# Twenty-four weight units get their high part by a converting transfer on GpSimd's queue, where VectorE copied it before

## The chip, the cores and the metric

The kernel runs on one core of a Trainium2 chip. The metric is the device time of one execution in microseconds, the median of several runs.

## The reference, cut to what matters

Two layers, each of a half-step feed-forward block, a mixer and a second half-step feed-forward block, on 256 tokens of width 1024 in fp32:

```
for l in range(2):
    x = x + 0.5 * swiglu(rmsnorm(x, ffn1_norm[l]), ffn1_w_up[l], ffn1_w_down[l])   # 1024 -> 2*2816 -> 1024
    p = rmsnorm(x, mix_norm[l]) @ w_in[l]
    p_rwkv, p_ga, p_wa, p_gate = split(p)             # 1920, 768, 768 and 3*1024 columns
    y_a = rwkv_mixer(p_rwkv, ...)                     # a scan over the tokens in both directions
    y_b = global_attention(...)                       # from p_ga
    y_c = window_attention(...)                       # from p_wa
    g = sigmoid(p_gate)                               # three gates of 1024
    merged = g0 * (y_a @ w_o_rwkv[l]) + g1 * (y_b @ w_o_ga[l]) + g2 * (y_c @ w_o_wa[l])
    x = x + merged @ w_out[l]
    x = x + 0.5 * swiglu(rmsnorm(x, ffn2_norm[l]), ffn2_w_up[l], ffn2_w_down[l])
return rmsnorm(x, final_norm)
```

## The kernel before

**Weights in units.** Every large matmul works on weight units of 128x1024 fp32 numbers (512 KB), made by `unit()`. A unit is loaded into `w_raw` by SyncE's queue (L80, three buffers). Its high part `w_hi` is the copy that rounds to fp32r (L91, four buffers): on ScalarE this copy is recorded at L61, on VectorE, as a CAST, at L63. Its low part `w_lo` is raw minus high (L92, four buffers), on VectorE or on GpSimd. Activations are held as a high and a low part too, and `mm3` makes each product from three matmuls: high by high, high by `w_lo`, and low by high. All these matmuls stand at L51, so the profile tells them apart by their output: `up` and `dn` in the feed-forward blocks, and in the mixer `pj` (queries, keys and values), `rk` (RWKV projections), `gt` (gates) and `wo` (output projections).

**Who makes which part.** In the feed-forward blocks ScalarE makes the high part and VectorE the low part. In the mixer the string `ENG` has a letter per unit for the engine pair: `v` ScalarE and VectorE, `p` ScalarE and GpSimd, `w` VectorE and GpSimd, `x` VectorE for both. `Mixer.on` turns the letter into the pair. Kind Q is the projection of queries, keys and values (12 units), R the RWKV projections, F the gates and the three output projections. In each layer twelve units have an `x`: Q1, Q2, Q3 and Q6, R6, and F3, F12, F13, F22 (of `w_o_wa`), F26, F32 and F33 (both of `w_o_rwkv`).

**The mixer's order.** The string `ORDER` interleaves generators: Q, R and F units, the attention steps, and the chunks of the RWKV scan. A scheduler then sets the order on each engine; each engine works through its own instructions in that order, and an instruction that waits holds up all behind it. Each layer's chunk work has a serial piece on VectorE: products of PSUM with masks (L743, L744: `LAt`, `LRt`), 32-wide transposes (L767), a substitution in pairs of small operations on `sol` (L775, L776: a multiply and an add), and the transpose into `Tn` (L785). TensorE then takes `Tn` to make `gp` and `tp` (32x32 matmuls), `hb`, `bonp` and `gatep`, among which it has `gt` matmuls. The gates' products are added into `merged` at L972 and L973. The RWKV projection is scaled into `RKV` at L611 and L612.

**GpSimd.** At the start of a mixer it makes the norm's statistics (L142 to L145), then issues six small transfers for the attention's constants (L393 to L397), and from these makes tables (L401, L407). Behind them stands its first `w_lo`. Later it makes some 30 `w_lo` per layer and small steps between.

Of the kernel before, what the change touches and what calls it, by code (L numbers as in the profile page):

```python
# [28 lines left out]
class Net:  # L29
# [38 lines left out]
    def unit(self, *srcs, on="av", turn=False):  # L68
        nc = self.nc
        raw = self.wp.tile([128, 1024], F32, name="w_raw", tag="w_raw", bufs=NRAW)  # L70
        c = 0
        for s in srcs:
            shp = s.shape
            n = 1
            for d in shp[1:]:
                n *= d
            dst = raw[:, c:c + n]
            if len(shp) == 3:
                dst = dst.rearrange("p (k c) -> p k c", k=shp[1])
            nc.sync.dma_start(out=dst, in_=s)  # L80
            c += n
        hi = self.wp.tile([128, 1024], F32R, name="w_hi", tag="w_hi", bufs=NHI)
        lo = self.wp.tile([128, 1024], F32R, name="w_lo", tag="w_lo", bufs=NLO)

        for i in range(2 if turn else 1):
            if turn:
                r = raw.rearrange("p (k w d c) -> p k w d c", w=2, d=2, c=64)[:, :, i]
                h, o = (x.rearrange("p (k d w c) -> p k d w c", w=2, d=2, c=64)[:, :, :, i] for x in (hi, lo))
            else:
                r, h, o = raw[:, :c], hi[:, :c], lo[:, :c]  # L90
            self.copy(on[0], h, r)  # L91
            self.engine(on[1]).tensor_tensor(o, r, h.bitcast(F32), ALU.subtract)  # L92
        return hi, lo

# [172 lines left out]


ORDER = 'QQQQQRRQQQRRQAQQRRRAAKAQRRPARRAKRKPVAVAARFRARFPVVAAAAAVAAVFAAFPAPFFVFFV00FFF01FF11F1001F01000000110F01F0F010PF1211F122PFFP112F1O3F32F3FFFO332323O223322F322232FF23323333OOOFFFFF'
ENG = {'Q': 'vxxxvvxppvvv', 'R': 'pvvwvpxvvvvvvvv', 'F': 'ppvxppppppppxxpppwpvvvxwwpxpppppxxwp', 'M': 'vvpvpvvv', 'O': 'vpvvpvvv', 'T': 'vaaaaaaaaaavavaa', 'G': 'vavaaa'}  # L270
KAP = float(np.exp(-0.5))
R_MU, R_W0, R_A0, R_KK, R_KA, R_RK, R_LG, R_LB, R_N = 0, 15, 23, 31, 35, 39, 43, 47, 51
PARTS = [("rwkv_mu", 15), ("rwkv_w0", 8), ("rwkv_a0", 8), ("rwkv_k_k", 4), ("rwkv_k_a", 4), ("rwkv_r_k", 4), ("rwkv_lnx_g", 4), ("rwkv_lnx_b", 4)]
# [15 lines left out]
class Mixer:  # L289
# [48 lines left out]
    def take(self, kind):  # L338
        s = ENG[kind]
        self.nlo[kind] = i = self.nlo.get(kind, -1) + 1  # L340
        return s[i % len(s)]
# [2 lines left out]
        return self.n.engine(self.take(kind))  # L344

    def on(self, kind):
        return {"v": "av", "p": "ap", "w": "vp", "x": "vv"}[self.take(kind)]


    def proj(self, c0, res, kind, first=False):  # L350
# [708 lines left out]
```

## Time and profile before

| | |
|---|---|
| runs | 1503.72, 1504.91 and 1505.63 us, median 1504.91 |
| the profiled execution | 1505.69 us, its span 1503.8 us, mean granted TensorE clock 0.98 |
| TensorE busy | 1425.9 us, 95% of the span |
| VectorE busy | 925.7 us, 62% |
| ScalarE busy | 701.9 us, 47% |
| GpSimd busy | 224.5 us, 15% |
| transfers | 220.19 MB, 146 GB/s over the span |

The mixers run from about 195 to 530 us and from about 940 to 1275 us of the span; the rest is feed-forward work. A time in the trace is counted from the span's start. A row's bracket gives the idle time of the engine ahead of it and what released it. TensorE's busy time includes waiting in its pipeline, so it is read with the gaps beside it.

### The profile page before, as it was taken

How to read it: one execution, taken by the hardware profiler on the slowest of the kernel's cores; microseconds unless marked ns; L12 is line 12 of the kernel's file. 1: busy time of each engine (PE TensorE's matmuls, PEld its weight loads, DVE VectorE, ACT ScalarE, POOL GpSimd, SP SyncE). 2: the span in 40 equal slices, each digit the busy share in tenths (PEclk: the TensorE clock that was granted, in tenths of full speed). 3: DMA queues.
4: the chain of work that ended last, by engine and by line, in shares of the span. 5: the costliest groups of instructions: out<-in, count | busy, mean ns of one | idle time of the engine just before them, and what ended most of it. 6: DMA issues, size and time to landing. Idle time of an engine off the chain costs nothing.

```text
span 1503.8 us, 25092 instructions
## 1 busy us (share of the span) xinstructions
PE 1425.9 (95%) x10170; PEld 1167.8 (78%) x10170; DVE 925.7 (62%) x1384; ACT 701.9 (47%) x1109; POOL 224.5 (15%) x203
## 2 busy tenths in 40 slices
PE   8999999999797999999999999999997979999997
PEld 6888878877575778888888888788785758788886
DVE  5455468765859666555465554778657685755543
ACT  6444335764333246444354443466642332554443
POOL 0000033223214110000000000432242132100001
PEclk9999999999899899999999999999998989999999
DMA  7666656323313146666666666553242121576653
GB/s 220 195 198 189 189 149 187 109 85 106 106 51 98 53 133 182 185 181 190 186 182 184 182 185 193 152 170 105 78 125 87 44 86 58 153 213 182 194 182 112
DMA packets 113432, 220.19 MB, mean 146 GB/s; under 512 B 7362, under 2 KB 32164, under 8 KB 113316
## 3 DMA queue, kind: packets, MB, share of 16 engines
q1 hardware_dynamic: 111328, 215.08, 47.7%
q10 hardware_dynamic: 1508, 2.58, 0.6%
q8 instruction: 80, 1.31, 0.4%
q0 software_dynamic: 480, 0.93, 0.3%
q14 instruction: 36, 0.29, 0.1%
HBM read 217.51 MB, written 1.05 MB: 145 GB/s over the span
## 4 chain that ended last, share of the span: by engine, by line
PE 69%; DVE 14%; issue 5%; ACT 5%; DMA 4%; POOL 3%; SPq 0%; POOLq 0%; ACTq 0%; DVEq 0%
PE up L51 26%; PE dn L51 18%; PE gt L51 5%; DMA w_raw<-in_ffn_w_up 3%; DVE w_lo L92 3%; PE rk L51 3%; PE tp L54 2%; PE wo L51 2%; PE yv L51 2%; ACT w_hi L61 1%; DVE sol L775 1%; PE tx L51 1%; DVE sol L767 1%; DVE sol L776 1%; PE pj L51 1%
## 5 line engine op out<-in xcount | busy, mean ns | idle before, releaser
L92 DVE TENSOR_TENSOR w_lo<-w_raw,w_hi 128x1024 fp32r<-128x1024 f32 (+1 forms) x348 | 427.0, 1229 | 343.3 <-ACT w_hi L61 342.4
L61 ACT ACTIVATE w_hi<-w_raw 128x1024 fp32r<-128x1024 f32 (+1 forms) x376 | 394.6, 1051 | 469.1 <-PE up L51 175.0
L51 PE MATMUL up<-w_hi,hT 128*128 128x512 f32 x1408 | 443.5, 394 | 0.0
L51 PEld LDWEIGHTS up<-w_hi,hT 128*128 128x128 f32 x1408 | 265.3, 189 | 53.9
L51 PE MATMUL up<-w_lo,hT 128*128 128x512 f32 x704 | 274.5, 391 | 0.0
L51 PE MATMUL dn<-w_hi,aT 128*128 128x512 f32 x704 | 218.2, 390 | 0.0
L92 POOL TENSOR_TENSOR w_lo<-w_raw,w_hi 128x1024 fp32r<-128x1024 f32 (+1 forms) x62 | 147.5, 2383 | 228.1 <-ACT w_hi L61 146.1
L51 PEld LDWEIGHTS up<-w_lo,hT 128*128 128x128 f32 x704 | 132.7, 188 | 28.2 <-DVE w_lo L92 1.1
L51 PEld LDWEIGHTS dn<-w_hi,aT 128*128 128x128 f32 x704 | 131.7, 188 | 26.8
L51 PE MATMUL dn<-w_lo,aT 128*128 128x512 f32 x352 | 138.0, 392 | 0.0
L51 PE MATMUL gt<-w_hi,hT 128*128 128x512 f32 x384 | 135.8, 418 | 2.3 <-DVE w_hi L63 2.3
L51 PE MATMUL rk<-hT,w_hi 128*128 128x256 f32 x480 | 88.2, 285 | 2.5 <-DVE RKV L611 2.5
L51 PEld LDWEIGHTS gt<-w_hi,hT 128*128 128x128 f32 x384 | 73.8, 195 | 20.6 <-issue 3.0
L51 PE MATMUL gt<-w_lo,hT 128*128 128x512 f32 x192 | 80.5, 419 | 2.5 <-DVE w_lo L92 2.5
L142 POOL TENSOR_SCALAR stat<-stat 128x1 f32<-128x1 f32 x14 | 3.5, 254 | 511.1 <-ACT gh L138 495.0
L51 PEld LDWEIGHTS rk<-hT,w_hi 128*128 128x128 f32 x480 | 75.3, 191 | 4.4 <-DVE RKV L611 2.9
L51 PEld LDWEIGHTS dn<-w_lo,aT 128*128 128x128 f32 x352 | 66.1, 188 | 14.8 <-DVE w_lo L92 1.4
L51 PE MATMUL rk<-hT,w_lo 128*128 128x256 f32 x240 | 67.9, 284 | 1.4 <-POOL w_lo L92 1.4
L51 PE MATMUL wo<-w_hi,yT 128*128 128x512 f32 x192 | 65.5, 407 | 0.0
L51 PE MATMUL pj<-w_hi,hT 128*128 128x512 f32 x192 | 62.0, 397 | 2.1 <-DVE LG L611 2.1
L51 PEld LDWEIGHTS rk<-hT,w_lo 128*128 128x128 f32 x240 | 45.8, 191 | 1.8 <-POOL w_lo L92 1.8
L51 PEld LDWEIGHTS gt<-w_lo,hT 128*128 128x128 f32 x192 | 37.5, 195 | 11.6 <-DVE w_lo L92 3.2
(238 smaller groups left out, 1833.8 us busy)
## 6 DMA issues: line engine op xcount, KB each, us to landing
w_raw<-in_ffn_w_up SPq DMA_DIRECT2D x160, 512.0 KB
w_raw<-in_w_in SPq DMA_DIRECT2D x102, 512.0 KB
w_raw<-in_ffn_w_down SPq DMA_DIRECT2D x88, 512.0 KB
w_raw<-in_ffn_w_up SPq DMA_DIRECT2D x32, 256.0 KB
w_raw<-in_w_out SPq DMA_DIRECT2D x16, 512.0 KB
w_raw<-in_w_o_ga SPq DMA_DIRECT2D x8, 512.0 KB
w_raw<-in_w_o_wa SPq DMA_DIRECT2D x8, 512.0 KB
w_raw<-in_w_o_rwkv SPq DMA_DIRECT2D x8, 512.0 KB
```

What stands on the lines that cost most here:

```text
L51: return self.nc.tensor.matmul(*a, **k)
L54: return self.nc.tensor.transpose(*a, **k)
L61: self.nc.scalar.activation(out, in_, AF.Copy, scale=1.0 if scale is None else scale)
L92: self.engine(on[1]).tensor_tensor(o, r, h.bitcast(F32), ALU.subtract)
L142: nc.gpsimd.tensor_scalar(self.ss[:, c:c + 1], self.ss[:, c:c + 1], 1.0 / D, EPS, ALU.mult, ALU.add)
L767: V.transpose(sol[p0:p0 + 32], src[p0:p0 + 32, :, 32 * b:32 * b + 32].rearrange("p g (u t) -> p t u g", u=2))
L775: V.tensor_tensor(tv, Dm[:, s + 1:16, s:s + 1].to_broadcast([128, m, s]), Dm[:, s:s + 1, 0:s].to_broadcast([128, m, s]), ALU.mult)
L776: V.tensor_tensor(Dm[:, s + 1:16, 0:s], Dm[:, s + 1:16, 0:s], tv, ALU.add)
```

## The change

A new letter `d` takes the place of `x` at all twelve places per layer, 24 in all. For such a unit, GpSimd issues a second transfer from the same place in DRAM, into `w_hi`, whose type (fp32r) differs from the source's, so that the transfer converts. VectorE's copy of the unit is left out. The low part is made by VectorE as before; it now waits for both transfers. The ten CASTs of letter `w` stay. Each of the new transfers moves 512 KB in 256 runs of 2 KB (128x2x512; R6's in 512 runs of 1 KB), and by the buffers of `w_hi` it waits for the matmuls that read its buffer's last unit. Lines behind the new code stand 8 further down: L92 is now L100.

```
         hi = self.wp.tile([128, 1024], F32R, name="w_hi", tag="w_hi", bufs=NHI)
         lo = self.wp.tile([128, 1024], F32R, name="w_lo", tag="w_lo", bufs=NLO)
+        if on[0] == "d":
+            c = 0
+            for s in srcs:
+                k = s.shape[1]
+                n = k * s.shape[2]
+                nc.gpsimd.dma_start(out=hi[:, c:c + n].rearrange("p (k c) -> p k c", k=k), in_=s)
+                c += n
...
-            self.copy(on[0], h, r)
+            if on[0] != "d":
+                self.copy(on[0], h, r)
             self.engine(on[1]).tensor_tensor(o, r, h.bitcast(F32), ALU.subtract)
...
-ENG = {'Q': 'vxxxvvxppvvv', 'R': 'pvvwvpxvvvvvvvv', 'F': 'ppvxppppppppxxpppwpvvvxwwpxpppppxxwp', ...
+ENG = {'Q': 'vdddvvdppvvv', 'R': 'pvvwvpdvvvvvvvv', 'F': 'ppvdppppppppddpppwpvvvdwwpdpppppddwp', ...
...
-        return {"v": "av", "p": "ap", "w": "vp", "x": "vv"}[self.take(kind)]
+        return {"v": "av", "p": "ap", "w": "vp", "x": "vv", "d": "dv"}[self.take(kind)]
```

**GpSimd at the start of the first mixer.** The norm's steps on `stat` for the second half of the tokens, and the attention's transfers behind them, before:

```order
L145 TENSOR_TENSOR stat_68<-stat_68 128x1
L142 TENSOR_SCALAR stat_68<-stat_68 128x1
L144 TENSOR_SCALAR stat_68<-stat_68 128x1
L145 TENSOR_TENSOR stat_68<-stat_68 128x1
L393 DMA at2_1580<-c_rope 128x2x128
```

and now, where `w_hi_1625`, `w_hi_1637` and `w_hi_1649` are the units Q1, Q2 and Q3:

```order
L153 TENSOR_TENSOR stat_68<-stat_68 128x1
L89 DMA w_hi_1625<-in_w_in 128x2x512
L150 TENSOR_SCALAR stat_68<-stat_68 128x1
L89 DMA w_hi_1637<-in_w_in 128x2x512
L89 DMA w_hi_1649<-in_w_in 128x2x512
L152 TENSOR_SCALAR stat_68<-stat_68 128x1
L153 TENSOR_TENSOR stat_68<-stat_68 128x1
L401 DMA at2_1580<-c_rope 128x2x128
```

The three transfers stand between the norm's steps and ahead of the attention's transfers.

**VectorE ahead of the substitution, first mixer.** `w_hi_4286` and `w_lo_4287` are the parts of unit F26. Before:

```order
L973 TENSOR_TENSOR merged_2937<-merged_2937,gth_4067 128x512
L743 TENSOR_TENSOR LAt_3872<-Lp0_4202,consts_494 128x256
L744 TENSOR_TENSOR LRt_4157<-Lp0_4202,consts_494 128x4x64
L743 TENSOR_TENSOR LAt_3872<-Lp1_4203,consts_494 128x256
L744 TENSOR_TENSOR LRt_4157<-Lp1_4203,consts_494 128x4x64
L63 CAST w_hi_4286<-w_raw_4284 128x1024
L767 STREAM_TRANSPOSE sol_4354<-LAt_3872 32x512
L92 TENSOR_TENSOR w_lo_4287<-w_raw_4284,w_hi_4286 128x1024
L63 COPY LRt_4157<-T1_4246 64x8x64
```

and now:

```order
L981 TENSOR_TENSOR merged_2937<-merged_2937,gth_4067 128x512
L751 TENSOR_TENSOR LAt_3872<-Lp0_4202,consts_494 128x256
L752 TENSOR_TENSOR LRt_4157<-Lp0_4202,consts_494 128x4x64
L751 TENSOR_TENSOR LAt_3872<-Lp1_4203,consts_494 128x256
L752 TENSOR_TENSOR LRt_4157<-Lp1_4203,consts_494 128x4x64
L100 TENSOR_TENSOR w_lo_4287<-w_raw_4284,w_hi_4286 128x1024
L775 STREAM_TRANSPOSE sol_4354<-LAt_3872 32x512
L63 COPY LRt_4157<-T1_4246 64x8x64
```

The CAST is gone and the low part has its place. Likewise the CAST of F32, which stood right ahead of the transposes into `Tn` at the end of the substitution, is gone there, and F32's low part has moved from between `Tn` and its use to behind the step that follows `tp` (L799). GpSimd issues F26's transfer ahead of the `w_lo` that starts at 453.47 us in the trace of before. In the second mixer F26's low part stands at the place of its CAST, four pairs of `LAt` and `LRt` earlier than before.

**TensorE at the use of Tn, first mixer.** `w_lo_4802` and `w_hi_4801` are the parts of another gate unit:

```order
 L51 MATMUL gt0_4699<-w_hi_4801,hT0_65 128x512
+L51 MATMUL gp_4394<-Tn_4392,LAt_3872 32x32 x32
+L51 MATMUL gp_4430<-Tn_4428,LAt_3872 32x32 x32
+L51 MATMUL tp1_4464<-sol_4354,Tn_4392 32x32 x32
+L51 MATMUL tp1_4503<-sol_4354,Tn_4428 32x32 x32
+L54 MATMUL hb_4542<-head_67,pz_4147 128x128 x4
 L51 MATMUL gt0_4699<-w_lo_4802,hT0_65 128x512
 L51 MATMUL gt0_4699<-w_hi_4801,hT1_66 128x512
```

The `gp`, `tp` and `hb` matmuls stand five `gt` matmuls earlier, so these five come behind `hb` now. In the second mixer three are moved so.

## Rows read from the trace of the kernel before

**Rows 1.** The page: busy time by engine, and the chain of work that ended last, by engine.

```profile
PE 1425.9 (95%) x10170; PEld 1167.8 (78%) x10170; DVE 925.7 (62%) x1384; ACT 701.9 (47%) x1109; POOL 224.5 (15%) x203
PE 69%; DVE 14%; issue 5%; ACT 5%; DMA 4%; POOL 3%; SPq 0%; POOLq 0%; ACTq 0%; DVEq 0%
```

**Rows 2.** Busy time of each engine in four stretches: stretch, its length, then busy us (and instructions) of PE, PEld, DVE, ACT and POOL, then the granted clock, the share of the DMA engines and GB/s.

```profile
462.00:490.00 28.00, 19.06 (x137) 14.76 (x129) 26.93 (x55) 8.62 (x11) 14.81 (x7) 0.92 0.36 113
490.00:498.00 8.00, 6.75 (x265) 6.22 (x266) 4.86 (x10) 3.14 (x8) 0.56 (x1) 0.50 0.21 70
1195.00:1225.00 30.00, 24.11 (x205) 18.34 (x204) 28.72 (x57) 8.23 (x11) 14.39 (x7) 0.97 0.34 106
1225.00:1234.00 9.00, 4.56 (x259) 4.39 (x260) 4.93 (x13) 2.54 (x5) 3.76 (x2) 0.50 0.21 62
```

**Rows 3.** VectorE's CASTs at L63: shortest, median and longest in ns, then the first and the last start.

```profile
L63 DVE CAST w_hi<-w_raw x34: 669/693/1977, 200.6 to 1257.3; 128x1024 fp32r<-128x1024 f32 x34
```

**Rows 4.** VectorE's timeline ahead of `Tn` in the first mixer: start, us, what.

```profile
463.92 2.83 DVE L973 TENSOR_TENSOR merged<-merged,gth 128x512 f32<-128x512 f32 x1
...
468.00 1.98 DVE L63 CAST w_hi<-w_raw 128x1024 fp32r<-128x1024 f32 x1
...
470.88 1.17 DVE L92 TENSOR_TENSOR w_lo<-w_raw,w_hi 128x1024 fp32r<-128x1024 f32 x1
...
477.67 2.36 DVE L776 TENSOR_TENSOR sol<-sol 128x36 f32<-128x36 f32 x1
...
480.30 0.20 DVE L776 TENSOR_TENSOR sol<-sol 128x44 f32<-128x44 f32 x1
...
488.92 0.67 DVE L63 CAST w_hi<-w_raw 128x1024 fp32r<-128x1024 f32 x1
```

**Rows 5.** GpSimd's timeline in the same stretch.

```profile
463.82 2.38 POOL L92 TENSOR_TENSOR w_lo<-w_raw,w_hi 128x1024 fp32r<-128x1024 f32 x1 [1.20 <-PE Lp L51]
467.08 2.35 POOL L92 TENSOR_TENSOR w_lo<-w_raw,w_hi 128x1024 fp32r<-128x1024 f32 x1 [0.87 <-ACT w_hi L61]
```

**Rows 6.** TensorE's timeline in the same stretch and up to the use of `Tn`.

```profile
470.04 0.51 PE L51 MATMUL gt<-w_hi,hT 128*128 128x512 f32 x1 [2.27 <-DVE w_hi L63]
472.10 0.79 PE L51 MATMUL gt<-w_lo,hT 128*128 128x512 f32 x1 [1.56 <-DVE w_lo L92]
472.69 1.05 PE L51 MATMUL gt<-w_hi,hT 128*128 128x512 f32 x2
473.55 0.63 PE L51 MATMUL gt<-w_lo,hT 128*128 128x512 f32 x1
...
481.07 0.63 PE L51 MATMUL gt<-w_hi,hT 128*128 128x512 f32 x2
481.54 0.39 PE L51 MATMUL gt<-w_lo,hT 128*128 128x512 f32 x1
...
490.08 1.93 PE L51 MATMUL gp<-Tn,LAt 32*32 32x32 f32 x128 [5.19 <-DVE Tn L785]
```

**Rows 7.** The same place in the second mixer: VectorE's timeline.

```profile
1202.49 1.17 DVE L63 CAST w_hi<-w_raw 128x1024 fp32r<-128x1024 f32 x1
...
1208.19 3.17 DVE L92 TENSOR_TENSOR w_lo<-w_raw,w_hi 128x1024 fp32r<-128x1024 f32 x1
...
1216.87 2.22 DVE L775 TENSOR_TENSOR sol<-sol 128x14 f32<-128x14 f32 x1
```

**Rows 8.** GpSimd's and then TensorE's timeline there.

```profile
1201.45 1.66 POOL L973 TENSOR_TENSOR merged<-merged,gth 128x512 f32<-128x512 f32 x1 [3.22 <-DVE gth L972]
...
1207.89 2.39 POOL L92 TENSOR_TENSOR w_lo<-w_raw,w_hi 128x1024 fp32r<-128x1024 f32 x1 [1.17 <-ACT w_hi L61]
...
1227.83 1.93 PE L51 MATMUL gp<-Tn,LAt 32*32 32x32 f32 x128 [7.42 <-DVE Tn L785]
```

**Rows 9.** The transfers: the queue that carries the weights (packets, MB, share of the 16 engines' span), and the issues from GpSimd's queue (count, KB each, median us from issue to landing).

```profile
q1 hardware_dynamic: 111328, 215.08, 47.7%
...
at<-c_rope POOLq DMA_DIRECT2D x4, 128.0 KB, 2.6
...
at<-in_ga_k_norm POOLq DMA_DIRECT2D x2, 32.0 KB, 5.2
```

**Rows 10.** GpSimd's timeline at the start of the first mixer.

```profile
202.22 0.30 POOL L142 TENSOR_SCALAR stat<-stat 128x1 f32<-128x1 f32 x1 [4.91 <-ACT gh L138]
204.57 0.79 POOL L144 TENSOR_SCALAR stat<-stat 128x1 f32<-128x1 f32 x1 [2.06 <-ACT gh L138]
...
208.04 1.70 POOL L393 DMA_DIRECT2D at<-c_rope  x2 [2.04 <-PE tp L54]
```

**Rows 11.** VectorE's timeline at the start of the first mixer, and at unit R6.

```profile
200.64 0.69 DVE L63 CAST w_hi<-w_raw 128x1024 fp32r<-128x1024 f32 x1 [0.18 <-PE dn L51]
...
204.02 1.21 DVE L92 TENSOR_TENSOR w_lo<-w_raw,w_hi 128x1024 fp32r<-128x1024 f32 x1
...
253.77 0.47 DVE L611 SCALAR_TENSOR_TENSOR RKV<-rk,par,projpad 128x256 f32<-128x256 f32 x1
```

**Rows 12.** TensorE's timeline at the same two places.

```profile
205.29 0.50 PE L51 MATMUL pj<-w_lo,hT 128*128 128x512 f32 x1 [1.11 <-DVE w_lo L92]
...
220.88 0.39 PE L51 MATMUL rk<-hT,w_lo 128*128 128x256 f32 x1 [0.79 <-POOL w_lo L92]
...
254.30 0.50 PE L51 MATMUL rk<-hT,w_hi 128*128 128x256 f32 x2 [1.29 <-DVE RKV L611]
```

More of the change, by code (lines that the diff above doesn't have):

```diff
@@ L269 @@
 ORDER = 'QQQQQRRQQQRRQAQQRRRAAKAQRRPARRAKRKPVAVAARFRARFPVVAAAAAVAAVFAAFPAPFFVFFV00FFF01FF11F1001F01000000110F01F0F010PF1211F122PFFP112F1O3F32F3FFFO332323O223322F322232FF23323333OOOFFFFF'
-ENG = {'Q': 'vxxxvvxppvvv', 'R': 'pvvwvpxvvvvvvvv', 'F': 'ppvxppppppppxxpppwpvvvxwwpxpppppxxwp', 'M': 'vvpvpvvv', 'O': 'vpvvpvvv', 'T': 'vaaaaaaaaaavavaa', 'G': 'vavaaa'}
+ENG = {'Q': 'vdddvvdppvvv', 'R': 'pvvwvpdvvvvvvvv', 'F': 'ppvdppppppppddpppwpvvvdwwpdpppppddwp', 'M': 'vvpvpvvv', 'O': 'vpvvpvvv', 'T': 'vaaaaaaaaaavavaa', 'G': 'vavaaa'}
 KAP = float(np.exp(-0.5))
```

## The prediction

> **What bounds the kernel now.** The page comes first: TensorE is busy 95% of the span, and the chain that ended last is 69% TensorE and 14% VectorE [rows 1]. So a microsecond counts only where TensorE stands idle; VectorE's 34 CASTs, 0.693 us each at the median [rows 3], cost nothing by themselves. Next come the stretches: ahead of the use of `Tn`, TensorE is busy 19.06 of 28 us and VectorE 26.93; in the second mixer VectorE is busy 28.72 of 30 us [rows 2]. There VectorE sets the time. The timelines show how: TensorE waits 5.19 us for `Tn` in the first mixer [rows 6] and 7.42 us in the second [rows 8], and VectorE has hardly a gap before that. Its pieces are of two kinds: work of the chain, and unit work that stands in the same queue (a CAST of 1.98 us at 468.00, a low part at 470.88, a CAST at 488.92 [rows 4]; a low part of 3.17 us at 1208.19 [rows 7]). Only the second kind can leave.
>
> Some of these pieces are three times as long as their like. The CAST at 468.00 ends at 469.98, just after GpSimd's `w_lo` that runs from 467.08 to 469.43; the merge at 463.92 ends 0.55 us after that of 463.82 to 466.20 [rows 4, 5]; the low part at 1208.19 ends at 1211.36, after GpSimd's from 1207.89 to 1210.28 [rows 7, 8]. A VectorE operation that reads SBUF twice, or the fp32 CAST, waits out a GpSimd `w_lo` that started before it. By the Trainium skill, "SBUF — State Buffer", section "Who interferes with whom", such an instruction and a GpSimd one that reads SBUF exclude each other for the whole instruction. The trace agrees.
>
> **The change, part by part.** *The price of a transfer.* No row shows a converting transfer. The nearest is `c_rope`: as many runs as most of the new ones (256), a quarter of the bytes, 2.6 us from issue to landing [rows 9]. The weights' queue moved 215.08 MB in 47.7% of the span, 300 GB/s [rows 9], so the other 384 KB take 1.3 us: **3.9 us**, an estimate. Lower bound 2.6 us (more bytes cost nothing); upper bound 6.5 us: `ga_k_norm`, of 32 KB, took 5.2 us among other traffic [rows 9], plus 1.3. I take 3.9, since `c_rope` has the same number of runs. On GpSimd one issue takes 0.85 us (two in 1.70 [rows 10]), and I bound it by 0.5 and 1.7 us for R6's 512 runs. By the Trainium skill, "DMA: Bandwidth & Descriptors", section "Anatomy of one DMA — SWDGE (gpsimd) path", a transfer of 512 KB would take about 2.0 + 1.2 = 3.2 us; by it the losses at Q1 and R6 below would vanish and the sum be 1.4 us lower.
>
> *F26 and F32, first mixer.* The CAST at 468.00 goes, 1.9 us of queue (the next starts at 469.90); that at 488.92 goes, 0.6 us. F26's transfer is issued near 452.3 us, lands near 456 and is not waited for. ScalarE's high part for GpSimd's `w_lo` of 463.82 now stands ahead of other work, so that `w_lo` can start about 1 us earlier and the merge at 463.92 wait about 1.0 us less. The low part of F26 then starts near 467 and runs into GpSimd's next `w_lo`: about 0.4 us lost. `Tn` comes 1.9 + 0.6 + 1.0 - 0.4 = 3.1 us earlier. Bounds: 1.3 us, if the low part is stretched as the CAST was (the CASTs' natural 0.69 + 0.6 alone); 5.7 us, if the stall at 477.67 (2.36 us against 0.20 for its like [rows 4]) also goes. I take it to stay, since a `w_lo` of GpSimd will meet some step of the substitution. TensorE's own stalls for F26 (2.27 and 1.56 us [rows 6]) go too, but they lie ahead of the 5.19 us of waiting for `Tn`: they only lengthen that wait.
>
> *What is given back.* Five `gt` matmuls that ran in front of `gp` now come behind `hb`, where TensorE is busy. At full clock two and one of them are 0.47 us apart (481.07 to 481.54), at half clock 0.86 us (472.69 to 473.55) [rows 6], so five cost 1.2 to 2.2 us. The granted clock is 0.50 from 490 to 498 us, the lower level (1.2 GHz), after the idle 5 us [rows 2]; how long it stays there with five large matmuls more I can't tell, so I take 1.6. Net in the first mixer: -1.5 us. F32's low part now stands behind `tp`'s step, in front of the second transposes: 0.3 us (0 to 0.6), since TensorE has other matmuls there.
>
> *F26, second mixer.* The low part of 3.17 us at 1208.19 leaves the front of the transposes. It takes the CAST's place (1202.49), where it waits for GpSimd's merge to end at 1203.11 as the CAST did, and ends 0.6 us later than the CAST; the merge on VectorE behind it waits for a `w_lo` anyway and swallows most of that. `Tn` 2.8 us earlier (0.5 to 5). Three `gt` matmuls move behind `hb`: 0.7 to 1.3 us, taken 1.0, since the clock stands at 0.50 there too [rows 2]. Net -1.8 us.
>
> *Q1 to Q3, at the start of each mixer.* Q1's transfer can start at 200.64, when TensorE frees the buffer (the CAST started then [rows 11]). It lands near 204.5; its low part started at 204.02 [rows 11], and TensorE waited 1.11 us for that [rows 12]. So TensorE is 0.5 us later, and with it the `tp` that releases `c_rope` at 208.04 [rows 10], on which GpSimd's chain to the first `w_lo` hangs, for which TensorE waits at 220.88 [rows 12]: **+0.5 us in each layer**, +1.0 (0 at 3.4 us of landing, +3.1 each at 6.5). The transfers also stand ahead of the statistics on GpSimd: from 202.22 to 204.57 there is room for two issues of 0.85 us [rows 10], nothing lost. The CASTs of Q2 and Q3 gone is nothing won: the wait at 220.88 is GpSimd's.
>
> *R6.* Its issue stands behind a `w_lo` of GpSimd that ends at 248.83; it lands near 252.7, its low part ends near 253.95, and the `RKV` step that released TensorE (at 253.77, TensorE at 254.30 after 1.29 idle [rows 11, 12]) waits behind it: +0.2 us per layer, +0.4 (-0.6 to +2.8 each). Q6, F3, F12, F13, F22 and F33 are used well after they land, or stand where TensorE has no gap: 0; that cover fails above about 5 us of landing.
>
> **Sum:** -1.5 + 0.3 - 1.8 + 1.0 + 0.4 = -1.6 us. From the profiled execution, 1505.69, that gives 1504.1; the median of the runs stands 0.8 lower, 1504.9, so the forecast is **1503.3 us**. Its own range is 1499.5 to 1505.5. A measurement of this kernel can tell about 0.2%, 3.0 us, from no change: "faster" begins at 1501.9, "slower" at 1507.9.
>
> **Rivals.** *Late landing (slower).* If the converting transfer takes 6 us or more, VectorE's queue stands at the low part that waits for it, and all behind it. Price at 6 us: +2.6 at Q1 and +2.3 at R6 per layer, 9.8 in place of 1.4, against gains of 3.0 that stay: 1504.9 + 9.8 - 3.0 = 1511.7. It decides from about 4.3 us of landing on, where it cancels the gains, and is slower by 3 us at 5.05. For it: 32 KB took 5.2 us [rows 9]. Against: Q1's and R6's bytes are few beside other traffic then, and `c_rope` took 2.6. By the Trainium skill, "SBUF — State Buffer", section "SBUF: two separate sides", GpSimd can't write descriptors while VectorE runs a copy in its two-port mode, so that the transfer stands still meanwhile. The two issues of 1.70 us beside VectorE's work [rows 10] show no such halt. Chance 0.22.
>
> *More is won (faster).* The stalls behind GpSimd's `w_lo` vanish rather than re-form, the landing is 3.3 us: `Tn` 5.7 and 5 us earlier, less 2.6: -8.1, 1496.8; half of it, 1500.5, is likelier. For it: the stalls depend on who starts first. Against: GpSimd is busy 14.81 of the 28 us [rows 2], so that some step of VectorE's will meet it. Chance 0.28.
>
> *Nothing is won (no change).* The low part stays stretched as the CAST was (1.3 us in the first mixer), the five matmuls cost 2.2: 1505 to 1506. Chance 0.12. That the transfer would not replace the CAST is excluded: VectorE's CASTs at L63 fall from 34 to 10 in the built order.
>
> The forecast keeps 0.38. Faster by over 0.2%: 0.10 of the forecast's and 0.25 of the second rival's, 0.35; slower: 0.20 of the first rival's and 0.03 of the third's, 0.23; within 0.2%: the rest, 0.42. The range, 1498.0 to 1508.5, leaves out the late landing above 5.2 us and the largest gains, about 0.2.
>
> **What would show it.** Right: 10 CASTs; issue to landing of `w_hi` near 3.9 us; the wait of `gp` for `Tn` still there, `gp` near 488 in the first mixer; TensorE's gap at 205 a little longer. Wrong: low parts on VectorE released by the transfer after long idle; issues over 1.7 us; `gp` at 490 or later.

## The result, and the profile after

The change made the kernel slower. The median is 1525.73 us (four runs, 1521.09 to 1528.70) against 1505.27 us before (four runs, one more than in the table of the kernel before, 1503.72 to 1505.78): ratio 1.0136, 95% interval 1.0119 to 1.0153, or about 20 us. The forecast was 1503.3 us with a range of 1498.0 to 1508.5; the result lies far outside, on the slow side, to which 0.23 had been given. The profiled execution of after took 1525.67 us, its span 1523.8.

The page and the list of TensorE's waits (engine, output and line <- what it waited for: us in all, times, longest) say first that TensorE does not work more, it stands longer. The page of after:

```profile
PE 1431.0 (94%) x10170; PEld 1173.9 (77%) x10170; DVE 910.4 (60%) x1360; ACT 703.0 (46%) x1109; POOL 240.5 (16%) x227
```

The three waits that matter here, of before and then of after:

```profile
PE gp L51 <- DVE Tn L785: 27.2, 4, 7.4
PE pj L51 <- DVE w_lo L92: 3.4, 6, 1.1
PE rk L51 <- DVE RKV L611: 2.5, 2, 1.3
```

```profile
PE gp L51 <- DVE Tn L793: 27.8, 4, 7.3
PE pj L51 <- DVE w_lo L100: 12.1, 4, 5.7
PE rk L51 <- DVE RKV L619: 6.4, 2, 3.4
```

VectorE's busy time fell by 15 us against [rows 1], as 24 CASTs are gone, and the time still rose. TensorE's wait of `pj` for a low part grew from 3.4 to 12.1 us and that of `rk` for `RKV` from 2.5 to 6.4; new in after are 3.1 us in which TensorE itself waits for a transfer into `w_hi`. The wait for `Tn`, at which the change's gain was expected, is as long as it was; around F26 `Tn` comes earlier, but so does TensorE.

*Where the 20 us are.* Both programs hold the same 10170 matmuls, so each one's start in after can be set against its start in before. The difference is called its lateness here. Where the median lateness of a stretch is larger than that of the stretch ahead of it, time is lost between the two. The table has these steps, in us, for the first and the second mixer:

| place | after | foreseen |
|---|---|---|
| start of the mixer, to 240 and 985 us | +9.1, +6.8 | +0.5, +0.5 |
| R6, at 254 and 1000 | +3.0, +3.6 | +0.2, +0.2 |
| F3, at 310 and 1060 | +0.8, +1.1 | 0, 0 |
| near 405 (an idle stretch and the clock behind it: last section) | -3.2, none | not foreseen |
| F26, up to the use of `Tn` | -4.7, -2.5 | -3.1, -2.8 |
| `hb` to the end, with F32 and F33 | +1.6, +3.2 | +1.9, +1.0 |

They add up to 18.8; a few steps of 0.3 to 0.6 elsewhere make 20.3.

**The start of the first mixer**, from the timeline of all engines (start, us, engine, line, operation; the bracket is the idle time ahead and what ended it):

```profile
205.64 1.23 DVE L100 TENSOR_TENSOR w_lo<-w_raw,w_hi 128x1024 fp32r<-128x1024 f32 x1 [1.42 <-DMA w_hi<-in_w_in]
...
205.75 0.47 PE L51 MATMUL pj<-w_hi,hT 128*128 128x512 f32 x1 [1.68 <-DMA w_hi<-in_w_in]
...
207.05 0.88 DVE L174 TENSOR_SCALAR gh<-x_res,stat 128x512 f32<-128x512 f32 x2
...
208.80 1.69 PE L54 MATMUL tp<-head,gh 128*128 128x128 f32 x8
...
210.78 1.51 POOL L401 DMA_DIRECT2D at<-c_rope  x2 [5.17 <-DVE hT L139]
...
220.81 1.82 DVE L455 TENSOR_TENSOR at<-att,at 128x256 f32<-128x256 f32 x2 [5.62 <-POOL at L415]
...
222.55 3.48 DVE L100 TENSOR_TENSOR w_lo<-w_raw,w_hi 128x1024 fp32r<-128x1024 f32 x3
...
224.88 0.79 PE L51 MATMUL pj<-w_lo,hT 128*128 128x512 f32 x1 [5.74 <-DVE w_lo L100]
```

Two things happen here. Q1's low part waits for its transfer until 205.64, 1.62 us later than in [rows 11]; `gh` is behind it in VectorE's queue, `tp` behind that on TensorE, and `c_rope` is issued at 210.78 where it was at 208.04 [rows 10]. The larger one ends in the last row: TensorE stands 5.74 us for a low part that VectorE starts only at 222.55, after 5.62 us of waiting for GpSimd's tables (L415). That low part belongs to Q4, a unit that the change doesn't touch. In the timeline of before VectorE made it first and waited for the tables afterwards:

```profile
212.81 1.23 DVE L92 TENSOR_TENSOR w_lo<-w_raw,w_hi 128x1024 fp32r<-128x1024 f32 x1 [0.87 <-ACT w_hi L61]
...
217.83 1.86 DVE L447 TENSOR_TENSOR at<-att,at 128x256 f32<-128x256 f32 x2 [2.68 <-POOL at L407]
```

So the built order of VectorE has changed. The low part (`w_lo_1690`) stood ahead of the first rotary products (`at2_1580`, steps of the attention) before:

```
L92 TENSOR_TENSOR w_lo_1690<-w_raw_1687,w_hi_1689 128x1024
L131 SCALAR_TENSOR_TENSOR hT1_66<-tp_1545,head_67,hT0_65 128x128
L131 SCALAR_TENSOR_TENSOR hT1_66<-tp_1559,head_67,hT0_65 128x128
L63 COPY att_1576<-pj0_1609 128x512
L447 TENSOR_TENSOR at2_1580<-att_1576,at3_1581 128x8x32 x2
```

and stands behind them now:

```
L139 SCALAR_TENSOR_TENSOR hT1_66<-tp_1559,head_67,hT0_65 128x128
L455 TENSOR_TENSOR at2_1580<-att_1576,at3_1581 128x8x32 x2
L100 TENSOR_TENSOR w_lo_1690<-w_raw_1687,w_hi_1689 128x1024
```

The second mixer has the same swap, with a gap of 4.93 us that ends at 975.03. The gaps cost twice: the granted clock is at its lower level (1.2 GHz) behind them, where the same stretches of before have 1.00. From the windows view (stretch, length, busy us and instructions of PE, PEld, DVE, ACT and POOL, then granted clock, share of the DMA engines, GB/s):

```profile
206.80:209.80 3.00, 2.88 (x9) 2.38 (x10) 2.25 (x5) 0.00 (x0) 0.00 (x0) 0.50 1.19 384
224.80:228.80 4.00, 3.92 (x9) 3.14 (x10) 1.23 (x3) 0.00 (x0) 0.00 (x0) 0.50 0.68 216
```

**The transfers**, from the view of the line that issues them (count, issue in ns shortest/median/longest):

```profile
L89 POOL DMA_DIRECT2D w_hi<-in_w_in x18: 713/753/958, 201.2 to 1217.1; - x18
...
  DVE w_lo L100: 41.2, 18
  PE pj L51: 3.1, 2
...
DMA to landing us min/median/max: 3.9/4.5/6.2
```

3.9 us is what the fastest needed, not the typical one. From issue to landing, Q1 to Q3 took 4.39, 5.63 and 6.23 us in the first mixer, R6 5.47 and 5.74, F3 5.57 and 5.71, F32 5.71 in the first mixer. Low parts on VectorE waited 41.2 us for them in all. An issue took 0.71 to 0.96 us, as reckoned (0.85).

**R6**, first mixer:

```profile
258.03 0.86 POOL L89 DMA_DIRECT2D w_hi<-in_w_in  x1
...
263.59 1.23 DVE L100 TENSOR_TENSOR w_lo<-w_raw,w_hi 128x1024 fp32r<-128x1024 f32 x1 [3.22 <-DMA w_hi<-in_w_in]
...
265.26 0.80 PE L51 MATMUL rk<-hT,w_hi 128*128 128x256 f32 x2 [2.98 <-DVE RKV L619]
```

TensorE's gap is 2.98 us where it was 1.29 [rows 12], and the matmuls behind it run at 0.80 us where they ran at 0.50: the granted clock fell there too (0.63 in the stretch from 265.20 to 269.20, 1.00 in before from 254.20 to 258.20).

**F26, F32 and F33.** From the timelines, where [rows 4, 6] answer for before:

```profile
473.75 1.59 DVE L981 TENSOR_TENSOR merged<-merged,gth 128x512 f32<-128x512 f32 x1
...
475.18 2.43 POOL L100 TENSOR_TENSOR w_lo<-w_raw,w_hi 128x1024 fp32r<-128x1024 f32 x1 [0.39 <-ACT w_hi L61]
...
476.60 2.10 DVE L100 TENSOR_TENSOR w_lo<-w_raw,w_hi 128x1024 fp32r<-128x1024 f32 x1
...
483.71 2.37 POOL L100 TENSOR_TENSOR w_lo<-w_raw,w_hi 128x1024 fp32r<-128x1024 f32 x1 [0.85 <-ACT w_hi L61]
483.80 2.56 DVE L778 SCALAR_TENSOR_TENSOR sol<-sol,consts 128x256 f32<-128x256 f32 x1
...
495.32 1.93 PE L51 MATMUL gp<-Tn,LAt 32*32 32x32 f32 x128 [6.41 <-DVE Tn L793]
502.32 1.23 DVE L100 TENSOR_TENSOR w_lo<-w_raw,w_hi 128x1024 fp32r<-128x1024 f32 x1 [2.41 <-DMA w_hi<-in_w_o_rwkv]
...
504.26 1.13 PE L51 MATMUL bonp<-pz,consts 128*128 128x256 f32 x4 [0.79 <-DVE sol L807]
...
1277.18 2.38 DVE L100 TENSOR_TENSOR w_lo<-w_raw,w_hi 128x1024 fp32r<-128x1024 f32 x1 [0.87 <-DMA w_hi<-in_w_o_rwkv]
...
1280.36 1.15 PE L51 MATMUL y<-LRt,Zt 128*64 128x64 f32 x32 [1.44 <-DVE ARV L852]
```

The merge is down from 2.83 to 1.59 us, the CAST of 1.98 is gone, and the low part is stretched to 2.10 by GpSimd's `w_lo`. `gp` starts 5.24 us later than before where it had been 9.84 late ahead of F26: 4.6 us won. Then F32's and F33's low parts, waiting for their own transfers, hold up steps of the scan.

### The profile page after: what moved, and what is told of

The parts are those of the page before. It is cut to its first block, busy times and chain, and to the rows that moved or that the text cites. A ratio compares the mean times of both kernels' runs of the same rounds, so it can differ in the third digit from the quotient of the medians.

```text
span 1523.8 us, 25136 instructions
## 1 busy us (share of the span) xinstructions
PE 1431.0 (94%) x10170; PEld 1173.9 (77%) x10170; DVE 910.4 (60%) x1360; ACT 703.0 (46%) x1109; POOL 240.5 (16%) x227
## 5 line engine op out<-in xcount | busy, mean ns | idle before, releaser
L100 DVE TENSOR_TENSOR w_lo<-w_raw,w_hi 128x1024 fp32r<-128x1024 f32 (+1 forms) x348 | 433.8, 1248 | 395.8 <-ACT w_hi L61 352.3
L100 POOL TENSOR_TENSOR w_lo<-w_raw,w_hi 128x1024 fp32r<-128x1024 f32 (+1 forms) x62 | 146.5, 2367 | 151.3 <-ACT w_hi L61 107.1
L51 PE MATMUL pj<-w_hi,hT 128*128 128x512 f32 x192 | 65.2, 414 | 5.4 <-DMA w_hi<-in_w_in 3.1
L51 PE MATMUL pj<-w_lo,hT 128*128 128x512 f32 x96 | 40.8, 429 | 12.3 <-DVE w_lo L100 12.1
L51 PEld LDWEIGHTS pj<-w_hi,hT 128*128 128x128 f32 x192 | 38.1, 200 | 15.0 <-ACT hT L135 3.9
```

Of the source, the lines that this page charges most:

```text
L51: return self.nc.tensor.matmul(*a, **k)
```

## The experiments

Three explanations were on the table after the two traces. Theory A: the order swap of Q4's low part costs most; transfers that land late while their low part stands in VectorE's queue cost the rest; F26 is a gain. Rival B: the swap is harmless, since TensorE would wait for GpSimd's first `w_lo` at that place anyway, and it is late transfers throughout. Rival C: the conversion makes the transfer slow.

All results, with the ratio to the kernel before on the same chip and its 95% interval (before: 1504.1 to 1504.8 us):

| run | us, median | ratio |
|---|---|---|
| e1, Q4's low part ahead again | 1517.31 | 1.0088 (1.0074 to 1.0102) |
| e2, before, Q4's low part behind | 1513.78 | 1.0064 (1.0051 to 1.0077) |
| e3, Q as before | 1515.41 | 1.0069 (1.0054 to 1.0085) |
| e4, F units alone | 1503.34 | 1.0000 (0.9989 to 1.0011) |
| e5, F26 alone | **1497.18** | 0.9953 (0.9939 to 0.9967) |
| e6, R6 alone | 1512.92 | 1.0059 (1.0045 to 1.0072) |
| e7, Q1 alone | 1500.53 | 0.9977 (0.9968 to 0.9987) |
| e8, Q2 and Q3 alone | 1511.88 | 1.0047 (1.0033 to 1.0061) |
| e9, e1 and Q1's low part behind `gh` | 1515.81 | 1.0069 (1.0048 to 1.0091) |
| e10, e9 and R6's low part behind `RKV` | 1519.20 | 1.0093 (1.0074 to 1.0112) |
| e11, plain transfer, VectorE copies | 1504.65 | one run |
| e12, F12, F13, F22 and F26 | 1499.31 | 0.9964 (0.9950 to 0.9978) |
| e13, R6 alone, low part on GpSimd | 1510.59 | 1.0036 (1.0025 to 1.0047) |

And the lateness of TensorE's matmuls by place, as in the table above (first, second mixer):

| run | start | after it, to R6 | R6 | near 405 | F26 |
|---|---|---|---|---|---|
| after | 9.1, 6.8 | -0.1, 0.3 | 3.0, 3.6 | -3.2 | -4.7, -2.5 |
| e1 | 4.3, 3.1 | -0.6, 2.5 | 3.6, 4.8 | -3.2 | -5.2, -2.5 |
| e2 | 6.1, 6.1 | -1.4, -1.3 | -0.4, -0.4 | -0.2 | 0, 0.2 |
| e3 | 0.1, 0 | 0.3, -0.1 | 4.5, 4.2 | 2.8 | -4.7, -2.6 |
| e4 | -0.3, 0.5 | 0.1, 0.1 | 0, 0 | -3.1 | -4.7, -2.5 |
| e5 | -0.1, 0.7 | -0.1, 0 | 0, 0 | -0.8 | -4.7, -2.5 |
| e6 | -0.3, 0.4 | 0.3, 0.2 | 3.4, 4.7 | -1.3 | |
| e7 | 0, 0.5 | -0.1, -0.1 | 0, 0.1 | -3.3 | |
| e8 | 5.7, 5.1 | -1.4, -1.3 | -0.4, -0.4 | -0.6 | |
| e9 | 1.1, 0.9 | 2.7, 2.5 | 1.6, 4.1 | -2.9 | -4.7, -2.5 |

**The swap, taken back (e1) and made alone (e2).** In e1 an edge in the scheduler's graph holds the first rotary product behind Q4's low part; two rows of VectorE per layer change place and nothing else. In e2 the kernel before gets the reverse edge; TensorE's matmuls with that low part move some places back with it.

```
+                if i == 1 and kp == 0:
+                    self.q4 = n.lo_ins
...
-                    tt(part(bh[:, h0:h1]), ... sn, ALU.mult)
+                    i = tt(part(bh[:, h0:h1]), ... sn, ALU.mult)
+                    if kind == 0 and t == 0 and h0 == 0:
+                        n.tc.add_manual_dep(i.ins, self.q4.ins.name, ...)   # e1; in e2 the other way round
```

> The changed kernel with one edge per layer that keeps VectorE's low part of unit Q4 ahead of the first two rotary products of the attention, as before the change; nothing else moves on any engine. Order theory (the scheduler's swap of these two makes most of the loss at a mixer's start): TensorE's gaps of 5.74 and 4.93 us go, TensorE then waits for GpSimd's low part behind the tables, which ends near 223.7 us; 11 to 12 us less, near 1514. Landing theory (Q1's transfer is late and all behind it is late with it, whatever the order): 0 to 2 us less, 1524 to 1526.

> The kernel before, with no new transfer, and one edge per layer that puts VectorE's low part of unit Q4 behind the first two rotary products, as in the changed kernel. Order theory: the low part starts near 219.6 us in place of 212.8, and TensorE, which wants it near 214, waits some 5 us in each layer: near 1514 to 1516. Landing theory: within 2 us of before, 1505 to 1507.

e1 gives back 7.2 us by the two ratios (8.4 by the medians, taken on two chips), e2 costs 9.5 us with no transfer changed. In the timeline of e2, the low part behind the first rotary products (L449, 218.23 to 220.06) releases TensorE as in after:

```profile
219.98 3.48 DVE L92 TENSOR_TENSOR w_lo<-w_raw,w_hi 128x1024 fp32r<-128x1024 f32 x3
222.31 0.80 PE L51 MATMUL pj<-w_lo,hT 128*128 128x512 f32 x1 [4.76 <-DVE w_lo L92]
```

and in that of e1 it is ahead of them (they start at 221.20), and only GpSimd's `w_lo` is waited for:

```profile
216.25 1.23 DVE L100 TENSOR_TENSOR w_lo<-w_raw,w_hi 128x1024 fp32r<-128x1024 f32 x1 [0.79 <-ACT w_hi L61]
...
224.22 0.39 PE L51 MATMUL rk<-hT,w_lo 128*128 128x256 f32 x1 [2.06 <-POOL w_lo L100]
```

That settles it against B: the swap is the largest piece, 7 to 9.5 us. e1 still missed its 1514 by 3 us: the gain at the start is 8.5 us instead of 11 to 12, and ahead of R6 and at R6 the second mixer loses 3.4 us more than in after.

**By kind: Q as before (e3), F alone (e4).** In e3 the Q units are copied by VectorE as before; in e4 Q and R6 both are.

```
-ENG = {'Q': 'vdddvvddpp...', 'R': 'pvvwvpdvv...', ...
+ENG = {'Q': 'vxxxvvxppvvv', 'R': 'pvvwvpdvv...', ...        # e3
+ENG = {'Q': 'vxxxvvxppvvv', 'R': 'pvvwvpxvv...', ...        # e4
```

> The changed kernel with the four Q units per layer back to VectorE's copy; R6 and the F units keep the transfer. Both theories: the 9.1 and 6.8 us that the matmuls slip at the two mixers' starts go, near 1509.5 to 1510; R6's slip of 2.8 and 3.6 us stays. If it is near 1505 or below, R6's slip hangs on what the Q units do.

> Q and R units back to VectorE's copy, the seven F units per layer keep the transfer. Theory (losses at Q and R6, gains at F26 given back in part behind F32 and F33): 1501 to 1504. Rival (the transfers as such cost time, through the memory or the shared DMA engines, wherever they stand): 1507 or more, since 14 of the 24 transfers remain.

e4 came as foreseen, no change: what F26 wins, F3, F32 and F33 give back. Its rival, that the transfers cost time wherever they stand, fell with it. e3 missed by 5 us. Its R6 costs 4.5 and 4.2 us, more than the 2.8 and 3.6 that I had taken over from after, and it loses 2.8 us near 405, where after gains 3.2.

**Single units: F26 (e5), R6 (e6), Q1 (e7), Q2 and Q3 (e8).** The edits are again letters of `ENG`: `x` everywhere but at the unit named, which keeps `d`.

```
+ENG = {'Q': 'vxxxvvxppvvv', 'R': 'pvvwvpxvv...', 'F': 'ppvxppppppppxxpppwpvvvxwwpdpppppxxwp', ...   # e5
+ENG = {'Q': 'vxxxvvxppvvv', 'R': 'pvvwvpdvv...', 'F': 'ppvxppppppppxxpppwpvvvxwwpxpppppxxwp', ...   # e6
+ENG = {'Q': 'vdxxvvxppvvv', ...   # e7, R and F with x
+ENG = {'Q': 'vxddvvxppvvv', ...   # e8, R and F with x
```

> Of all 24 units only F26 of each layer keeps the transfer; all others are copied by VectorE as before. Theory (F26 is the one place that wins, 4.7 us in the first and 2.5 us in the second mixer in the three traces so far; F32 and F33 give back 1.4 and 3.2 because their transfers hold VectorE's queue): 1496 to 1498.5, faster by 6 to 8 us. Rival (the gain is given back behind Tn by the matmuls that the order moves there, whoever makes F32's high part): 1501 to 1504.

> Only R6 of each layer keeps the transfer; TensorE's, ScalarE's and GpSimd's own work stand exactly as before. Head-of-line theory: the low part waits until landing, 5.5 to 6.5 us after issue, and the RKV step behind it releases TensorE 4 to 5 us late in each layer: 1512 to 1515. If the R6 slip of the changed kernel was a follow of the Q units: within 2 us of before.

> Only Q1 of each layer keeps the transfer; the scheduler leaves the low part of Q4 ahead of the rotary products. Landing theory for Q1: it lands 4.2 to 4.4 us after issue, TensorE is 1 to 2 us late, runs a while at half clock, and the tp that releases c_rope is late: 2 to 3 us per layer, 1508 to 1510. Rival (Q1's lateness is swallowed by the wait at GpSimd's first low part): 1505 or less.

> Only Q2 and Q3 of each layer keep the transfer; the scheduler again puts the low part of Q4 behind the rotary products. Order theory: the same loss as the kernel before with that swap alone, 9 to 10 us: 1513 to 1515. Rival (Q2 and Q3 landing late adds to it): 1517 or more.

e5 is the best version of all, 6.9 us faster than before and faster than the change by 28. F26's transfer took 5.0 and 5.1 us there, and only one of the two low parts waited for it, 0.8 us.

e6: two transfers cost 8.9 us. The order on TensorE and ScalarE is that of before, so this is the late part alone, 3.49 us of VectorE's waiting and a gap of 3.24 us on TensorE, in the timeline of e6:

```profile
248.72 0.85 POOL L89 DMA_DIRECT2D w_hi<-in_w_in  x1
248.80 8.92 SPq L80 DMA_DIRECT2D w_raw<-in_w_in  x3
...
254.54 1.22 DVE L100 TENSOR_TENSOR w_lo<-w_raw,w_hi 128x1024 fp32r<-128x1024 f32 x1 [3.49 <-DMA w_hi<-in_w_in]
256.22 0.50 PE L51 MATMUL rk<-hT,w_hi 128*128 128x256 f32 x2 [3.24 <-DVE RKV L619]
```

The SPq row is SyncE's queue: the first of these three weight loads is issued 0.08 us behind R6's transfer (more on this at e11).

e7 missed: Q1 alone costs nothing. There the scheduler put Q1's low part behind `gh`, so that the wait for the transfer holds nobody in VectorE's queue; `tp` is on time (timeline of e7; 206.67 in before):

```profile
205.84 0.88 DVE L174 TENSOR_SCALAR gh<-x_res,stat 128x512 f32<-128x512 f32 x2 [0.48 <-POOL stat L153]
206.47 1.06 PE L54 MATMUL tp<-head,gh 128*128 128x128 f32 x8 [0.18 <-DVE gh L174]
206.63 1.22 DVE L100 TENSOR_TENSOR w_lo<-w_raw,w_hi 128x1024 fp32r<-128x1024 f32 x1
```

Its gain is no merit of the transfer: 3.3 us of it come near 405, as in after, at no place that Q1 touches. e8 has the swap again, and its cost: 5.7 and 5.1 us; its time is a little under the 1513 to 1515 foreseen. So changing Q2 and Q3 is enough to make the scheduler swap, and changing Q1 alone is not.

**Q1's low part behind `gh` in the whole change (e9), and R6's behind `RKV` (e10).** Two more edges on top of e1.

```
+                if i == 0 and kp == 1:
+                    n.tc.add_manual_dep(n.lo_ins.ins, n.gh_ins.ins.name, ...)            # e9, e10
...
+                    if (g, j0, ku) == (1, 2, 1):
+                        n.tc.add_manual_dep(n.lo_ins.ins, self.step.ins.name, ...)       # e10
```

> All 24 transfers, the low part of Q4 ahead of the rotary products (as in the first experiment), and one more edge per layer: the low part of Q1, which waits for its transfer, stands behind the two norm scalings into gh, for which TensorE's tp and by it the c_rope transfers wait. Head-of-line theory (Q1's landing costs only by what VectorE has queued behind it): c_rope goes out 2 us earlier, 2 to 3 us less per layer than the first experiment, 1511 to 1514 against its 1517. Landing theory (TensorE itself lacks Q1's parts): within 1.5 us of 1517.

> All 24 transfers with three edges per layer: the two of the experiment before, and the low part of R6 behind the RKV step (L619) that TensorE waits for; this moves some of the attention's steps on VectorE and ScalarE too. Head-of-line theory: R6's 4 to 5 us per layer go, 1501 to 1505, level with the kernel that has the F units alone. Rival (the transfers' bytes cost time by themselves): 1508 or more.

e9 shows the cause of Q1's loss by the place and not by the total: the lateness at the start falls from 4.3 and 3.1 us to 1.1 and 0.9 (some `pj` matmuls and one copy of ScalarE move with the edge). With e1's edge, two changes of order explain 8.0 of 9.1 us in the first mixer and 5.9 of 6.8 in the second. But the time fell by only 1.5 us against e1 (2.9 by the ratios), which is what the landing theory had foreseen for the total, since 2.7 and 2.5 us come back ahead of R6: the wait for `LG` is longer (2.22 us; 1.08 in before), in the timeline of e9:

```profile
228.91 1.23 DVE L100 TENSOR_TENSOR w_lo<-w_raw,w_hi 128x1024 fp32r<-128x1024 f32 x1 [6.17 <-DMA w_hi<-in_w_in]
230.29 0.48 DVE L625 SCALAR_TENSOR_TENSOR LG<-rk,par,projpad 128x256 f32<-128x256 f32 x1 [0.16 <-ACT projpad L624]
...
244.37 0.51 PE L51 MATMUL pj<-w_hi,hT 128*128 128x512 f32 x1 [2.22 <-DVE LG L625]
```

Q6's low part waits 6.17 us there with the `LG` steps behind it. But the first of these then waits 0.16 us more, for ScalarE's `projpad`, which stands behind a copy that waits 8.17 us for its own load (6.60 in before). Which of the two makes the gap was not tested. e10 missed by far. R6's gap did break up (into 0.81 and 0.53 us in the first mixer), but the edge changed the scheduler's order elsewhere, and a new gap came up (timeline of e10; 1.51 us in the other kernels):

```profile
290.05 1.97 PE L54 MATMUL hb<-head,kkrs 128*128 128x128 f32 x8 [3.63 <-ACT kkrs L650]
```

So e10 gives no price for R6.

**Is it the conversion? (e11)** The 24 units' raw fp32 part comes by a plain transfer on GpSimd's queue instead of SyncE's, and VectorE copies it as before.

```
-            nc.sync.dma_start(out=dst, in_=s)
+            (nc.gpsimd if on[0] == "d" else nc.sync).dma_start(out=dst, in_=s)
```

> For the price of the transfer alone: the same 24 units load their raw part by a plain fp32 transfer of GpSimd's queue, at other times than the converting ones, and VectorE copies the high part. If the conversion is what takes time, undisturbed plain ones land clearly under 3.9 us; if it is the queue and the bytes, at 3.8 to 4.2 us undisturbed. The kernel's time is not the point, somewhere over 1510.

```profile
DMA to landing us min/median/max: 3.9/4.1/5.1
```

The shortest is the same 3.9 us, with or without conversion, so C falls as far as an undisturbed transfer goes. The time, one run, is that of before, not the "over 1510" foreseen: 24 loads on GpSimd's queue cost nothing by themselves where VectorE keeps its copies.

The longest is 5.1 against 6.2. The traces show what goes with a late landing. The twelve kernels with converting transfers issue 146 of them. In 45 cases SyncE issues a weight load within 0.6 us behind the transfer, as in e6: all of these took 4.9 to 7.4 us, with a median of 5.5. Of the other 101 (median 4.1), 77 took less than 4.9, and 18 of the 24 later ones are Q2 or Q3, which are issued right behind one another. Of e11's 24 plain transfers one had such a load behind it, and it is the longest, 5.13 us. So a plain transfer can be late too. How busy the DMA engines are does not order them: their share was 0.77 while one of after landed in 4.08 us (380.70 to 384.80) and 0.78 while R6's took 5.47. This is a pattern in the traces; no run moved SyncE's load away to test it.

**Without F3, F32 and F33 (e12).**

```
+ENG = {'Q': 'vxxxvvxppvvv', 'R': 'pvvwvpxvv...', 'F': 'ppvxppppppppddpppwpvvvdwwpdpppppxxwp', ...
```

> F12, F13, F22 and F26 keep the transfer; F3, F32 and F33 are copied again. Theory (F3 costs 0.7, F32 and F33 1.5 and 3.2 us per layer, the other three nothing): 1496.5 to 1499, level with F26 alone and 5 to 6 us below all seven. Rival (the loss against F26 alone comes from F12, F13 or F22): 1501 or more.

Leaving the three out of e4 gives 4.0 us by the medians, 5.4 by the ratios; the stretches at F3, F32 and F33 had shown some 5 us lost. F12, F13 and F22 neither give nor take anything that shows: e12, just above its range, and e5 overlap (1493.67 to 1502.88, and 1496.54 to 1498.00).

**R6: the part, or the queue? (e13)** As e6, but GpSimd makes R6's low part, so VectorE's queue doesn't stand at it.

```
+ENG = {..., 'R': 'pvvwvpevv...', ...
-        return {..., "d": "dv"}[self.take(kind)]
+        return {..., "d": "dv", "e": "dp"}[self.take(kind)]
```

> Only R6 keeps the transfer, as in the experiment with R6 alone, but its low part is made by GpSimd, which has nothing else to do there; VectorE's queue then holds nothing that waits for the transfer, and TensorE's and ScalarE's order stay as they are. Head-of-line theory: the RKV step comes no later than before; TensorE waits only for the low part itself, which ends about 1 us after it is wanted: 1505 to 1508, 5 us or more below R6 alone. Rival (the late parts of R6 hold TensorE whoever makes them, or the transfer's traffic does): 1511 or more, as R6 alone.

It came out between the two, 2.6 us above the range of the head-of-line theory. From the timeline of e13:

```profile
252.42 0.48 DVE L619 SCALAR_TENSOR_TENSOR RKV<-rk,par,projpad 128x256 f32<-128x256 f32 x1
...
254.34 3.17 POOL L100 TENSOR_TENSOR w_lo<-w_raw,w_hi 128x1024 fp32r<-128x1024 f32 x1 [4.79 <-DMA w_hi<-in_w_in]
...
257.57 0.39 PE L51 MATMUL rk<-hT,w_lo 128*128 128x256 f32 x1 [2.68 <-POOL w_lo L100]
```

`RKV` is now early (253.77 before [rows 11]), so VectorE's queue is free, and TensorE waits for the low part itself. Both are late: what stands behind the low part, and the low part. Part of what is left is no matter of the transfer: GpSimd needs 3.17 us for the low part, VectorE 1.22 in e6.

## Why the prediction was wrong, point by point

- *"The CASTs of Q2 and Q3 gone is nothing won: the wait at 220.88 is GpSimd's."* This is the step that failed most. It asked whether the wait at 220.88 would shrink, not what takes the place of the CASTs. With them gone, the scheduler put the low part of Q4 behind a step that waits for GpSimd's tables: 7 to 8 us by e1, 9.5 us by e2. The swap stood in the built order before the run; I had followed only the units that the change touches.
- *Q1, +0.5 us in each layer.* Landing was nearly as reckoned (4.39 and 4.12 us against 3.9) and the low part began 1.6 us later. The mistake was to pass on 0.5 us: `gh` and then `tp` stand behind the low part, the clock is halved meanwhile (`tp` takes 1.69 us where it took 1.07 in before), and `c_rope` leaves 2.7 us late. 4.3 and 3.1 us in e1, 1.1 and 0.9 once the low part is behind `gh` (e9).
- *R6, +0.2 us per layer, up to +2.8.* The mechanism was right and the landing mis-sized: with its issue in the foreseen place (248.72 in e6, 248.83 foreseen), it landed after 5.5 and 5.7 us (5.7 to 5.8 in e6, 7.4 in e1's second mixer). The gap of 1.29 us grew to 2.98, and the clock fell behind it. 3.0 and 3.6 us in after, 8.9 us for both in e6. Why its lateness varies from 1.6 us (e9) to 4.8 (e1) is open.
- *Landing 3.9 us.* This is about the shortest seen (3.8 in e9), not a typical value; the upper bound of 6.5 us held in after (longest 6.2), but not in e1 (7.4) and e9 (7.7). By the Trainium skill, "DMA: Bandwidth & Descriptors", section "Anatomy of one DMA — SWDGE (gpsimd) path", an estimate of 3.2 us had been worked out; no landing in any run here was that short.
- *Late landing (slower), deciding from 4.3 us, 1511.7 at 6 us.* This rival was right in kind and I gave it too little: at its own terms, with R6 at 5.5 to 5.7 us and F3, F32 and F33 waited for as well, e1 without the swap is at 1517.3. Its ground against, that Q1's and R6's bytes are few beside other traffic, did not hold for R6: with a load of SyncE's issued some 0.08 us behind it, it took 5.4 to 7.4 us in all kernels that have it.
- *Q6, F3, F12, F13, F22, F33 at 0, "fails above about 5 us".* It failed for F3 (+0.8, +1.1) and F33, whose transfer took only 4.09 us but whose low part stood ahead of `ARV`; it held for F12, F13 and F22, and in after for Q6.
- *F26, -3.1 and -2.8.* Right in mechanism: -4.7 and -2.5. In the first mixer the merge shrank by 1.2 us (foreseen 1.0), CAST and stretched low part by 1.0 (foreseen 1.5), the missing CAST of F32 gave 0.4 (foreseen 0.6), and of two stalls inside the substitution (477.67 [rows 4], and 2.24 us at 484.24 in the same timeline) one did not re-form: 2.1 us that I took to stay. What was given back behind `hb` is 1.0 us in e5 (foreseen 1.6), where TensorE had already gained 1.3 more on the way there.
- *F32's low part, 0.3 us.* Its issue went behind a GpSimd `w_lo` and its landing took 5.71 us; the stretch costs 1.6 us in the first mixer and 3.2 us, with F33, in the second. In e5, without both, it gives nothing back.

By the Trainium skill, "SBUF — State Buffer", section "SBUF: two separate sides", issues could have stood still beside VectorE's copies; the longest issue in any run took 0.96 us, so no run shows an issue that was halted. Whether such a halt has a part in a late landing, the runs don't tell.

## What to carry to other kernels

When an engine loses instructions under a scheduler, read the whole built order around each place for rows of *other* work that changed sides of a waiting instruction: here one swapped row cost about as much as all the late transfers at that place (8.5 us of lateness that e1 takes back, 7.4 that stay). A transfer in place of a copy is paid by what stands in the queue behind its consumer, so replace a copy only where even a late landing (5 to 7.7 us here, not the undisturbed 3.9) lies well ahead of the consumer's turn. Of 24 replacements, the two of F26 alone gave 1497.18 us, faster than both kernels.

## What the runs showed that I had not expected

TensorE has idle stretches of up to 2.1 us (2.4 in e11) inside its runs of 32x32 matmuls that no engine ends. In the timeline of before:

```profile
407.63 0.20 PE L51 MATMUL gp<-Tn,LAt 32*32 32x32 f32 x1 [2.10 <-issue]
```

A packet of the instruction queue (16 KB) starts at 405.29, just ahead of it. After, e1, e4, e7 and e9 don't have this stretch; before, e2, e3, e5, e6, e8 and e10 to e13 do, and at different matmuls. That the loading of TensorE's program causes it was not tested.

How long the clock stays at its lower level behind such a place differs from kernel to kernel, with the same matmuls to run. The wait for `Tn` ends at 403.60 us in before, at 416.70 in after and at 408.86 in e3. Before is back at 1.00 from 415 on, after from 423 on, and e3 not until 425. Windows, the clock as the third number from the right; of before:

```profile
410.00:415.00 5.00, 5.00 (x43) 3.36 (x42) 2.15 (x3) 2.21 (x6) 0.00 (x0) 0.60 0.50 118
```

of after, and of e3:

```profile
418.00:423.00 5.00, 5.00 (x147) 4.05 (x141) 3.23 (x7) 1.66 (x4) 0.55 (x1) 0.63 0.27 68
```

```profile
420.00:425.00 5.00, 5.00 (x68) 4.29 (x68) 2.66 (x4) 0.58 (x1) 0.00 (x0) 0.50 0.01 4
```

At this place a kernel's lateness moved by -3.3 to +2.8 us (after -3.2, e7 -3.3, e3 +2.8), more than several terms of my sum.

A converting transfer of 512 KB from GpSimd's queue lands after 3.8 us at best (a plain one after 3.9), and after 4.9 to 7.4 us where SyncE issues a load within 0.6 us behind it; `c_rope`'s median went from 2.6 us [rows 9] to 4.2.
